# Transposed h stays on chip in freed operand sets during the last gate product; row scales by halves of the tokens; other places for loads

## The chip, the cores and the metric

The kernel runs on one core of one Trainium2 chip. The metric is the time of one execution on the device in microseconds (us). The median of several executions is given, and one further execution is recorded by the hardware profiler.

## The reference, cut to what matters

```python
# x: 1 x 512 x 2048, all in float32; D_MODEL = 2048, PLE_DIM = 256
h = x
for i in range(2):
    xn = rms_norm(h, norm_pre[i])
    if i == 0:                       # layer AB: attention and a recurrent mix
        proj = xn @ ab_w_in[0]
        ...
        y = concat(...) @ ab_w_out[0]
    else:                            # layer C: gated MLP over chunks of tokens
        u, v, g = split(xn @ c_w_in[0], 3)
        oc = chunked_spatial_gating(u, v, c_ln_g, c_ln_b, c_w_s, c_b_s)   # gelu, layer norm, 16 groups
        y = (oc * silu(g)) @ c_w_out[0]
    h = h + rms_norm(y, norm_post[i])
    h = h + (p[i] @ ple_w_proj[i]) * sigmoid(h @ ple_w_gate[i])
return h
```

The change touches the second pass (i = 1): the mix of layer C in one place, and above all what follows c_w_out: the RMS norm of y, the product p @ ple_w_proj (the "filler") and the last gate product h @ ple_w_gate with the output behind it.

## The kernel before

Products in float32 are made of three matmuls on split operands (high times high, high times low, low times high). For each 128x512 piece of a weight, ScalarE (ACT) casts the high part `whi` (L1466), and VectorE (DVE) subtracts it to get the low part `wlo` (L1467); four buffers of each stand ahead of TensorE (PE).

From c_w_in on, the products use a scheme of seven half-sized products in place of eight (`seven`, with the weights made in `pieces`). A `Pair` stands for 1024 columns of the weight. In the gate product there are two, a (output blocks n = 0, 1) and b (n = 2, 3), and `FIRST` sets the order b1, a1, b2, a2, a5, a6, a3, a4, a7, b5, b6, b4, b7, b3. Each of these fourteen is eight ticks k of six matmuls (128x512), 48 in all. Each has an operand set made of sums of quarters of h: `s[1]` in xh0 and xh1 (called A11), and `SETS` gives the tiles of the others, so yl0 to yl7 for product 2, yl8 to yl15 for 5, xl for 6 and 3, yh for 7 and 4. A set is free once its products of both pairs are done.

Weights come on SP's DMA queue (`load` in `pieces`, L1417, 512 KB each) into eight piece buffers. Sums of two weight blocks are made by VectorE (L1425), or by a DMA that accumulates, issued by GpSimd (POOL; `grow`, L1421). Product 4 loads eight halves of 256 KB (L1459) and adds them on VectorE.

Around the products a clock counts ticks: `later(n, step)` hangs a step on the n-th tick from here, and a scheduler with priorities orders each engine's instructions. Each engine, SP's queue included, then runs its own in order.

In the mix of layer C, groups 0 to 15 each take back normed columns of v from the DRAM tile `vd` (write L1566, load L1589, tile `sq`, both on ACT's queue) and norm them on ACT (L1598). In c_w_out, `out_block` writes scaled copies of y (L1138) and their squares (L1141) and adds the squares of each half of the tokens, e = 0 or 1, into `accq[e]` on POOL (L1142; `accq[1]` is the tile rstdB). A matmul with ones sums them over partitions (L1220), and `row_rstd` makes the row scale with Ln and Exp (L369, L370) behind a load of their table (L367). `update(q, e)` (L1192, L1193) multiplies y by it and adds to h. `load` (L1156) brings h back from DRAM before.

The filler (L251 to L253, four groups of 24 matmuls) runs between c_w_out and the gate product. ACT copies its results (L1207) and writes them to the DRAM tile `pd` from ACT's own queue. `flip` transposes a block of h on TensorE (L1232, four transposes), copies it on ACT (L1234) and writes it to the DRAM tile `rd`. SP fetches pd (L1273) and rd (L1274) back for each output block, and `emit` makes the sigmoid (L1277), multiplies by pd's part (L1278), adds rd's (L1280) and writes the output (L1282).

Of the kernel before, what the change touches and what calls it, by code (L numbers as in the profile page):

```python
# [16 lines left out]
P = 128  # L17
# [78 lines left out]
class Pair:  # L96


    def __init__(self, W, c0, n, emit):
        self.W, self.c0, self.n, self.emit = W, c0, n, emit  # L100
        self.E, self.H, self.acc, self.R, self.done = {}, {}, {}, {}, set()


class Net:
# [911 lines left out]
    def run(self):  # L1016
        tc = self.tc
        with ExitStack() as ctx:
# [10 lines left out]
            self.pd, self.rd = (self.t(dp, [P, 4, D], n) for n in ("pd", "rd"))  # L1029
# [92 lines left out]
    def last_layer(self, cp, fs, turn, wp, ps):  # L1122
# [8 lines left out]
        def out_block(pr, m, n, src):  # L1131
# [7 lines left out]
            if seen[e]:  # L1139
                sq = self.t(wp, [P, T], "sq")  # L1140
                nc.scalar.activation(sq, src, AF.Square)  # L1141
                nc.gpsimd.tensor_tensor(accq[e], accq[e], sq, ALU.add)  # L1142
            else:
                nc.scalar.activation(accq[e], src, AF.Square)
            seen[e] = True

# [34 lines left out]
        steps += [(82, ple)]  # L1181
# [8 lines left out]
        def update(q, e):  # L1190
            r = self.rstdB[:, e * 256 : e * 256 + 256].unsqueeze(1).broadcast_to([P, 2, 256])
# [3 lines left out]
        def filler():  # L1195
            phi, plo = self.pops
            for g in range(4):
                if g == 1:
                    self.A11 = self.whole_set()
                for q in (2 * g - 2, 2 * g - 1) if g else ():  # L1200
                    update(q, 0)
                    if q < 4:
                        self.part(self.A11, q, H[q, 0])
                accs = self.dense_tm(i["ple_w_proj"][1], g * T, T, phi, plo, ps)
                for m in range(4):
                    pj = self.slot("xl", 4 * (g % 2) + m, F32)
                    nc.scalar.copy(pj, accs[m])  # L1207
                    nc.scalar.dma_start(self.pd[:, m, g * T : (g + 1) * T], pj)
                if g == 0:
                    yield  # L1210
            for q in (6, 7):
                update(q, 0)

        more = filler()
        next(more)
        with tc.high_priority(HP):
            pt = self.t(ps, [P, T], "mm")
            for e in range(2):
                for a in range(2):
                    nc.tensor.matmul(  # L1220
                        pt[:, e * 256 : e * 256 + 256], self.ones, accq[e][:, a * 256 : a * 256 + 256],
                        start=(a == 0), stop=(a == 1),
                    )
            self.row_rstd(pt, self.rstdB, self.last)
        for _ in more:
            pass

        def flip(g, m):
# [4 lines left out]
            o = self.slot("xl", g + 4 * m, F32) if m < 2 else self.t(wp, [P, T], ("sg", "sq")[m % 2])  # L1233
            nc.scalar.copy(o, pt)  # L1234
            nc.scalar.dma_start(self.rd[:, m, g * T : (g + 1) * T], o)

        s, sets, x2, s1, s24, s3, x22 = self.sums(H, wp, SETS)
        s[1] = self.A11
        for q in range(4):
            x2(q)  # L1240
        spare = [[], []]
# [6 lines left out]
        def early_spare():  # L1248
            for j in range(8):
                spare[j % 2].append(self.slot("yh", j, F32))  # L1250

        def late_spare():
            for j in range(2):
                tl = self.t(self.xp, [P, 4, T], f"xh{2 + j}")
                spare[j][:] = [tl[:, q, :] for q in range(4)]

        steps = [(1 + k, lambda g=g, m=m: flip(g, m)) for k, (g, m) in enumerate((g, m) for g in (2, 0, 3, 1) for m in (0, 1))]
        steps += [(2 + 4 * q, lambda q=q: late(q)) for q in range(4)]
        steps += [(16, early_spare)]
        steps += [(19 + 3 * q, lambda q=q: s24(q)) for q in range(4)]  # L1260
        steps += [(30 + k, lambda g=g, m=m: flip(g, m)) for k, (g, m) in enumerate((g, m) for g in (2, 0, 3, 1) for m in (2, 3))]
        steps += [(38 + q, lambda q=q: s3(q)) for q in range(4)]
        steps += [(43 + q, lambda q=q: x22(q)) for q in range(4)] + [(47, late_spare)]
        for n, step in steps:
            self.later(n, step)
        pj, res = {}, {}

        def fetch(n, ms):
            for m in ms:
                pj[n, m], res[n, m] = (x[0] for x in spare)  # L1270
                for x in spare:
                    x.append(x.pop(0))
                nc.sync.dma_start(pj[n, m], self.pd[:, m, n * T : (n + 1) * T])  # L1273
                nc.sync.dma_start(res[n, m], self.rd[:, m, n * T : (n + 1) * T])  # L1274
# [12 lines left out]
        order = FIRST(*pairs, (4, 7, 3))  # L1287

        def ahead(step):
            if step + 1 < len(order):  # L1290
                pr, prod, _ = order[step + 1]
                if prod == 2:
                    fetch(pr.n, (0, 1))
                elif prod == 3:
                    self.later(3, lambda: fetch(pr.n + 1, (0, 1)))
                elif prod == 7:
                    fetch(pr.n + 1, (2, 3))
# [684 lines left out]
```

## Time and profile before

| | us |
|---|---|
| runs | 2279.76, 2271.38, 2278.86 |
| median | 2278.86 |
| profiled execution | 2278.64 |
| its span | 2276.9 |
| TensorE busy in the span | 2218.1 (97%) |
| VectorE, ScalarE, GpSimd busy | 1559.8, 1271.3, 267.5 |

The span runs from the first to the last instruction that the profile shows; the execution's time is 1.7 us longer. Times in the profile's rows are from the span's start. In them c_w_in's part that matters lies at 1495 to 1546, the mix from about 1622, the end of c_w_out at 2054.5, the filler to 2081.4, the gate product from there to 2268.9, and the last outputs to 2276.9. Rows of a busy engine give its start, its length, the engine, the line, and in brackets its idle time and what ended it. Rows of waits give the total, the number and the longest.

### The profile page before, as it was taken

The numbers are of one execution on the slowest core, as the hardware profiler recorded it, in microseconds if no ns is written. First come the engines' busy times: TensorE is split into PE (matmuls) and PEld (weight loads), VectorE is DVE, ScalarE is ACT, GpSimd is POOL, SyncE is SP. The second block draws the span as 40 slices with busy tenths as digits, with TensorE's granted clock in tenths as the row PEclk, the third lists the DMA queues.
The fourth block names the chain that finished last, engine by engine and source line by source line (L and its number), as shares of the span: only waits on it lengthen the run. The fifth ranks groups of instructions, "written<-read, shape, count | busy, mean of one in ns | idle before, by whom it ended". The sixth has DMA issues, their size and how long they took to land.

```text
span 2276.9 us, 40608 instructions
## 1 busy us (share of the span) xinstructions
PE 2218.1 (97%) x15369; PEld 1842.4 (81%) x15369; DVE 1559.8 (69%) x3008; ACT 1271.3 (56%) x2594; POOL 267.5 (12%) x318
## 2 busy tenths in 40 slices
PE   8999999999999999999999999999999999998988
PEld 7878888888887888878888888878878779997766
DVE  8666667666643877872237448878688688877868
ACT  5455555555443777753244547546566667556644
POOL 2000010010100000000010112101111111321020
PEclk9999999999999999999999999999999999999999
DMA  7322232223234533343335436776867776687696
GB/s 232 91 78 73 69 86 81 73 67 84 75 98 134 163 101 98 102 149 97 98 102 165 133 119 165 194 202 162 202 181 188 200 182 162 159 222 238 196 253 187
DMA packets 299442, 322.19 MB, mean 142 GB/s; under 512 B 15677, under 2 KB 191454, under 8 KB 298222
## 3 DMA queue, kind: packets, MB, share of 16 engines
q1 hardware_dynamic: 250990, 255.62, 36.8%
q0 software_dynamic: 21760, 41.95, 10.7%
q10 hardware_dynamic: 26496, 22.03, 3.2%
q8 instruction: 121, 1.98, 0.4%
q14 instruction: 75, 0.61, 0.1%
HBM read 284.64 MB, written 34.90 MB: 140 GB/s over the span
## 4 chain that ended last, share of the span: by engine, by line
PE 77%; DVE 9%; DMA 8%; ACT 3%; issue 3%; SPq 0%; ACTq 0%; POOL 0%; DVEq 0%; POOLq 0%
PE mm L1502 22%; PE mm L210 11%; PE mm L212 10%; PE mm L211 10%; PE mm L992 4%; PE mm L994 4%; PE mm L993 4%; DVE wlo L1467 3%; DMA sq<-vd 2%; DVE rq L1425 1%; PE tm L548 1%; DMA half<-in_ple_w_gate_dram 1%; PE tm L569 1%; DMA rq<-in_ple_w_gate_dram 1%; DMA half<-in_c_w_in_dram 1%
## 5 line engine op out<-in xcount | busy, mean ns | idle before, releaser
L196 DVE TENSOR_TENSOR wlo<-raw,whi 128x512 fp32r<-128x512 f32 x400 | 284.5, 719 | 309.1 <-ACT whi L194 272.2
L194 ACT CAST whi<-raw 128x512 fp32r<-128x512 f32 x400 | 247.0, 619 | 346.2 <-PE mm L993 151.3
L211 PE MATMUL mm<-xl,whi 128*128 128x512 f32 x1056 | 415.4, 393 | 0.0
L210 PE MATMUL mm<-xh,whi 128*128 128x512 f32 x992 | 412.6, 416 | 0.0
L212 PE MATMUL mm<-xh,wlo 128*128 128x512 f32 x992 | 392.4, 396 | 0.0
L1466 ACT CAST whi<-rq 128x512 fp32r<-128x512 f32 x432 | 264.4, 620 | 208.7 <-PE mm L1502 126.1
L1467 DVE TENSOR_TENSOR wlo<-rq,whi 128x512 fp32r<-128x512 f32 x432 | 300.0, 705 | 109.8 <-ACT whi L1466 107.8
L211 PEld LDWEIGHTS mm<-xl,whi 128*128 128x128 f32 x1056 | 199.6, 189 | 32.3
L212 PEld LDWEIGHTS mm<-xh,wlo 128*128 128x128 f32 x992 | 186.6, 188 | 41.1
L210 PEld LDWEIGHTS mm<-xh,whi 128*128 128x128 f32 x992 | 187.4, 189 | 33.2
L1502 PE MATMUL mm<-whi,yh 128*128 128x512 f32 x512 | 163.5, 396 | 3.8 <-ACT whi L1466 3.8
L1502 PE MATMUL mm<-whi,xl 128*128 128x512 f32 x512 | 163.0, 394 | 2.8 <-ACT whi L1466 2.3
L1502 PE MATMUL mm<-whi,yl 128*128 128x512 f32 x512 | 163.4, 395 | 0.7 <-ACT whi L1466 0.7
L1502 PEld LDWEIGHTS mm<-whi,yh 128*128 128x128 f32 x512 | 97.4, 190 | 24.9 <-ACT whi L1466 4.6
L1502 PEld LDWEIGHTS mm<-whi,xl 128*128 128x128 f32 x512 | 96.9, 189 | 24.2 <-ACT whi L1466 3.1
L1502 PEld LDWEIGHTS mm<-whi,yl 128*128 128x128 f32 x512 | 97.1, 190 | 21.9 <-ACT whi L1466 1.5
L1467 DVE TENSOR_TENSOR wlo<-raw,whi 128x512 fp32r<-128x512 f32 x128 | 88.7, 698 | 32.6 <-ACT whi L1466 32.4
L1466 ACT CAST whi<-raw 128x512 fp32r<-128x512 f32 x128 | 78.5, 620 | 56.7 <-PE mm L1502 25.3
L1502 PE MATMUL mm<-wlo,yl 128*128 128x512 f32 x256 | 101.5, 396 | 8.8 <-DVE wlo L1467 8.8
L1502 PE MATMUL mm<-wlo,yh 128*128 128x512 f32 x256 | 101.6, 397 | 1.5 <-DVE wlo L1467 1.5
L1502 PE MATMUL mm<-wlo,xl 128*128 128x512 f32 x256 | 101.0, 394 | 1.9 <-DVE wlo L1467 1.9
L1502 PE MATMUL mm<-whi,xh 128*128 128x512 f32 x256 | 82.2, 398 | 2.8 <-ACT xl L1207 1.7
(518 smaller groups left out, 4680.8 us busy)
## 6 DMA issues: line engine op xcount, KB each, us to landing
raw<-in_ab_w_in_dram SPq DMA_DIRECT2D x128, 512.0 KB, 3.9
rq<-in_c_w_in_dram SPq DMA_DIRECT2D x50, 512.0 KB, 6.2
raw<-in_ple_w_gate_dram SPq DMA_DIRECT2D x42, 512.0 KB, 4.5
rq<-in_c_w_in_dram POOLq DMA_DIRECT2D x36, 512.0 KB, 8.0
raw<-in_ab_w_out_dram SPq DMA_DIRECT2D x32, 512.0 KB, 3.8
raw<-in_c_w_in_dram SPq DMA_DIRECT2D x26, 512.0 KB, 3.7
half<-in_c_w_in_dram SPq DMA_DIRECT2D x48, 256.0 KB, 3.4
rq<-in_c_w_out_dram SPq DMA_DIRECT2D x24, 512.0 KB, 13.0
```

What stands on the lines that cost most here:

```text
L194: nc.scalar.copy(hi[:, : m * n], src)
L196: self.weng.tensor_tensor(lo[:, : m * n], src, f(hi[:, : m * n]), ALU.subtract)
L210: nc.tensor.matmul(acc, hi, xhi[k], start=(k == 0), stop=False)
L211: nc.tensor.matmul(acc, hi, xlo[k], start=False, stop=False)
L212: nc.tensor.matmul(acc, lo, xhi[k], start=False, stop=(k == nk - 1))
L548: nc.tensor.matmul(px[dst, e, :], a[src, e, :], b[src, e, :], start=True, stop=True)
L992: nc.tensor.matmul(accs[j], hi[:, js], xhi[k], start=(k == 0), stop=False)
L993: nc.tensor.matmul(accs[j], hi[:, js], xlo[k], start=False, stop=False)
L994: nc.tensor.matmul(accs[j], lo[:, js], xhi[k], start=False, stop=(k == nk - 1))
L1466: nc.scalar.copy(hi, src)
L1467: nc.vector.tensor_tensor(lo, src, f(hi), ALU.subtract)
L1502: nc.tensor.matmul(o, x, y, start=(first and r == 0 and j == 0 and not a), stop=(r == 7 and j == 2), **more)
```

## The change

Five things are changed.

1. The DRAM tile rd is gone. The sixteen flips copy into tiles that products 1 and 2 have freed (xh0, xh1 and yl0 to yl7), and `emit` adds from there. They are also later: eight in b2 and a2, eight in a5, a6 and a3, where before eight stood in b1 and a1, and eight from a2 on.
2. The results of the filler go to pd on SP's queue, not ACT's, and are fetched in five groups at set ticks.
3. The row scale is made per half of the tokens: the first half within the last products of c_w_out (with a table load of its own), the second behind the first group of the filler. The updates of the first half, with the sums of operands that follow from them, partly stand in c_w_out now. Six of the additions of squares go from POOL to VectorE.
4. Product a4 takes its weights by four accumulating DMAs of 512 KB instead of eight half loads and eight additions.
5. In the mix, each load of `vn` (L1589 before, L1576 after) is tied to the latest weight cast.

The core of the diff:

```diff
+        def row_scale(e):
+            with tc.high_priority(HP):
+                pt = self.t(ps, [P, 256], "mm")
+                for a in range(2):
+                    nc.tensor.matmul(pt, self.ones, accq[e][:, a * 256 : a * 256 + 256], start=(a == 0), stop=(a == 1))
+                self.row_rstd(pt, accq[e][:, :256], self.last)
...
                 nc.scalar.activation(sq, src, AF.Square)
-                nc.gpsimd.tensor_tensor(accq[e], accq[e], sq, ALU.add)
+                eng = nc.vector if pr.n == 2 and n + e > 2 else nc.gpsimd
+                eng.tensor_tensor(accq[e], accq[e], sq, ALU.add)
...
-        steps += [(82, ple)]
+        steps += [(82, ple), (98, lambda: row_scale(0))]
...
         def update(q, e):
-            r = self.rstdB[:, e * 256 : e * 256 + 256].unsqueeze(1).broadcast_to([P, 2, 256])
+            r = accq[e][:, :256].unsqueeze(1).broadcast_to([P, 2, 256])
...
+        for g in range(4):
+            accs = self.dense_tm(i["ple_w_proj"][1], g * T, T, phi, plo, ps)
+            for q in (g, g + 4):
                 update(q, 0)
+            self.part(self.A11, g, H[g, 0])
+            for m in range(4):
+                pj = self.slot("xl", 4 * (g % 2) + m, F32)
+                nc.scalar.copy(pj, accs[m])
+                nc.sync.dma_start(self.pd[:, m, g * T : (g + 1) * T], pj)
+            x2(g)
+            if g == 0:
+                row_scale(1)
...
         def flip(g, m):
...
-            o = self.slot("xl", g + 4 * m, F32) if m < 2 else self.t(wp, [P, T], ("sg", "sq")[m % 2])
+            if m < 2:
+                if m == 0 and g % 2 == 0:
+                    self.fl = self.t(self.xp, [P, 4, T], f"xh{1 - g // 2}")
+                o = self.fl[:, g % 2 * 2 + m, :]
+            else:
+                o = self.slot("yl", 2 * g + m - 2, F32)
+            res[g, m] = o
             nc.scalar.copy(o, pt)
-            nc.scalar.dma_start(self.rd[:, m, g * T : (g + 1) * T], o)
...
+        def fetch(n, m, o):
+            pj[n, m] = o
+            nc.sync.dma_start(o, self.pd[:, m, n * T : (n + 1) * T])
+
+        def first_fetch(n):
+            for m in range(2):
+                fetch(n, m, self.t(self.wq, [P, T], f"half{m}") if n == 1 else self.slot("yh", 2 - n + m, F32))
+
+        def next_fetch():
+            for j, ns in enumerate(((1, 0), (3, 2))):
                 tl = self.t(self.xp, [P, 4, T], f"xh{2 + j}")
+                for k in range(4):
+                    fetch(ns[k // 2], 2 + k % 2, tl[:, k, :])
+
+        def last_fetch():
+            tl = self.t(self.xp, [P, 4, T], "xh2")
+            for m in range(2):
+                fetch(3, m, tl[:, m, :])
...
+        steps = [(1 + 6 * q, lambda q=q: late(q)) for q in range(4)]
+        for at, g, m in (
+            (17, 2, 0), (18, 2, 1), (20, 3, 0), (21, 3, 1), (23, 0, 0), (25, 0, 1), (27, 1, 0), (29, 1, 1),
+            (34, 2, 2), (36, 2, 3), (38, 0, 2), (40, 0, 3), (42, 1, 2), (44, 1, 3), (46, 3, 2), (48, 3, 3),
+        ):
+            steps.append((at, lambda g=g, m=m: flip(g, m)))
...
+        steps += [(5, lambda: first_fetch(2)), (14, lambda: first_fetch(0)), (36, lambda: first_fetch(1))]
+        steps += [(56, next_fetch), (90, last_fetch)]
...
+        pairs[0].whole = True
+        self.seven(FIRST(*pairs, (4, 7, 3)), Sets(nxt), ps)
...
+            elif pr.whole:
+                tl = done = pr.E.pop(j)
+                grow(tl, 1, 0, j)
...
-                    nc.scalar.copy(hi, src)
+                    self.cast = nc.scalar.copy(hi, src)
...
-                nc.scalar.dma_start(vn, self.vd[:, g])
+                with tc.issue_after(self.cast.ins):
+                    nc.scalar.dma_start(vn, self.vd[:, g])
```

In the places that follow, names ending in numbers are tiles, `whi`/`wlo` the split weights, `mm` PSUM tiles. The first place is TensorE in the filler. Before, the ones matmul for the second half stands within the filler's second group, behind 40 of its matmuls:

```order
L253 MATMUL mm_22617<-whi_22639,yl_4536_21953 128x512
L251 MATMUL mm_22618<-whi_22639,yl_4535_21952 128x512
L252 MATMUL mm_22618<-wlo_22640,yl_4535_21952 128x512
L1220 MATMUL mm_22599<-rstdB_12776,ones_119 128x256 x2
L251 MATMUL mm_22620<-whi_22623,yl_4531_21941 128x512
L252 MATMUL mm_22620<-wlo_22624,yl_4531_21941 128x512
L253 MATMUL mm_22620<-whi_22623,yl_4532_21942 128x512
```

After, it stands directly behind the filler's first group of 24:

```order
L251 MATMUL mm_22559<-whi_22578,yl_4534_21951 128x512
L252 MATMUL mm_22559<-wlo_22579,yl_4534_21951 128x512
L253 MATMUL mm_22559<-whi_22578,yl_4535_21952 128x512
L1152 MATMUL mm_22616<-rstdB_12775,ones_118 128x256 x2
L251 MATMUL mm_22622<-whi_22628,yl_4530_21940 128x512
L252 MATMUL mm_22622<-wlo_22629,yl_4530_21940 128x512
L253 MATMUL mm_22622<-whi_22628,yl_4531_21941 128x512
```

The sum of the second half has moved ahead of sixteen matmuls, and everything after it in the filler stands behind it.

The second place is SP's queue in the gate product, around the weights of b5 (the four 512 KB loads rq from ple_w_gate). Before, fetches of pd and rd and writes of the output stand between them:

```order
L1417 DMA rq_4988_23958<-in_ple_w_gate_dram 128x2x512
L1273 DMA xh_4922_23630<-pd_101 128x512
L1417 DMA rq_4993_23985<-in_ple_w_gate_dram 128x2x512
L1282 DMA out_dram<-xh_4923_23631 128x512
L1273 DMA xh_4922_23630<-pd_101 128x512
L1282 DMA out_dram<-xh_4923_23631 128x512
L1417 DMA rq_4998_24008<-in_ple_w_gate_dram 128x2x512
L1274 DMA xh_4923_23631<-rd_102 128x512 x2
L1417 DMA rq_5003_24031<-in_ple_w_gate_dram 128x2x512
```

After, eight fetches of pd stand together ahead of b5's weights, and a half load of b4 and two output writes between them:

```order
L1243 DMA xh_4932_23699<-pd_101 128x512 x4
L1243 DMA xh_4933_23704<-pd_101 128x512 x4
L1400 DMA rq_4972_23911<-in_ple_w_gate_dram 128x2x512
L1400 DMA rq_4977_23938<-in_ple_w_gate_dram 128x2x512
L1445 DMA half_5017_24108<-in_ple_w_gate_dram 128x512
L1280 DMA out_dram<-xh_4783_23144 128x512
L1400 DMA rq_4982_23961<-in_ple_w_gate_dram 128x2x512
L1280 DMA out_dram<-xh_4783_23144 128x512
L1400 DMA rq_4987_23984<-in_ple_w_gate_dram 128x2x512
```

The fetches of pd have moved ahead of the four weights, and those of rd are gone.

The third place is ACT in c_w_in. Before, the first two loads of v (`sq` from `vd`) stand among the weight casts, some fifty rows ahead of their norm (row L1598):

```order
L1466 CAST whi_16854<-rq_3440_16769 128x512
L1466 CAST whi_16864<-rq_3440_16769 128x512
L1589 DMA sq_17660<-vd_103 128x512
L1466 CAST whi_16890<-rq_3402_16603 128x512
L1589 DMA sq_17731<-vd_103 128x512
L1466 CAST whi_16900<-rq_3402_16603 128x512
L1466 CAST whi_16916<-rq_3407_16626 128x512
```

After, the first load stands some ninety rows later and two casts ahead of its norm (now L1585):

```order
L1452 CAST whi_17639<-rq_3521_17167 128x512
L1452 CAST whi_17649<-rq_3521_17167 128x512
L1576 DMA sq_17659<-vd_102 128x512
L1452 CAST whi_17667<-raw_17374 128x512
L1452 CAST whi_17677<-raw_17374 128x512
L1585 ACTIVATE sq_17659<-sq_17659,nb_15726,rv_15725 128x128 x3
L1452 CAST whi_17688<-raw_17397 128x512
```

The load has moved behind the writes of vd and close to its use.

More of the change, by code (lines that the diff above doesn't have):

```diff
@@ L99, in __init__ @@
     def __init__(self, W, c0, n, emit):
-        self.W, self.c0, self.n, self.emit = W, c0, n, emit
+        self.W, self.c0, self.n, self.emit, self.whole = W, c0, n, emit, False
         self.E, self.H, self.acc, self.R, self.done = {}, {}, {}, {}, set()
@@ L1028, in run @@
             self.hd = self.t(dp, [P, KT, T], "hd")
-            self.pd, self.rd = (self.t(dp, [P, 4, D], n) for n in ("pd", "rd"))
+            self.pd = self.t(dp, [P, 4, D], "pd")
             self.vd, self.yd2 = (self.t(dp, [P, c, 4, P], n) for n, c in (("vd", KT), ("yd2", 8)))
@@ L1190, in update @@
         def update(q, e):
-            r = self.rstdB[:, e * 256 : e * 256 + 256].unsqueeze(1).broadcast_to([P, 2, 256])
+            r = accq[e][:, :256].unsqueeze(1).broadcast_to([P, 2, 256])
             nc.vector.tensor_tensor(Y[q, e], Y[q, e], r, ALU.mult)
             nc.vector.tensor_tensor(H[q, e], H[q, e], Y[q, e], ALU.add)
[L1195 to L1211, printed above, removed]
-                update(q, 0)
[L1214 to L1226, printed above, removed]
+        self.A11 = self.whole_set()
+        nxt, _, x2, s1, s24, s3, x22 = self.sums(H, wp, SETS)
+        nxt[1] = self.A11
+        phi, plo = self.pops
+        for g in range(4):
+            accs = self.dense_tm(i["ple_w_proj"][1], g * T, T, phi, plo, ps)
+            for q in (g, g + 4):
+                update(q, 0)
+            self.part(self.A11, g, H[g, 0])
[6 more added lines that the diff above has]
+                row_scale(1)
+        pj, res = {}, {}
         def flip(g, m):
@@ L1232, in flip @@
                 nc.tensor.transpose(pt[:, j * P : (j + 1) * P], src, self.ident)
-            o = self.slot("xl", g + 4 * m, F32) if m < 2 else self.t(wp, [P, T], ("sg", "sq")[m % 2])
-            nc.scalar.copy(o, pt)
-            nc.scalar.dma_start(self.rd[:, m, g * T : (g + 1) * T], o)
[L1237 to L1241, printed above, removed]
+            if m < 2:
[5 more added lines that the diff above has]
+            res[g, m] = o
+            nc.scalar.copy(o, pt)
         def late(q):
@@ L1246, in late @@
             s1(q)
[L1248 to L1253, printed above, removed]
-                tl = self.t(self.xp, [P, 4, T], f"xh{2 + j}")
-                spare[j][:] = [tl[:, q, :] for q in range(4)]
-        steps = [(1 + k, lambda g=g, m=m: flip(g, m)) for k, (g, m) in enumerate((g, m) for g in (2, 0, 3, 1) for m in (0, 1))]
-        steps += [(2 + 4 * q, lambda q=q: late(q)) for q in range(4)]
@@ L1259, in last_layer @@
[L1259 to L1264, printed above, removed]
-            self.later(n, step)
[L1266 to L1274, printed above, removed]
+        def fetch(n, m, o):
+            pj[n, m] = o
+            nc.sync.dma_start(o, self.pd[:, m, n * T : (n + 1) * T])
@@ new lines, in last_layer @@
+        steps = [(1 + 6 * q, lambda q=q: late(q)) for q in range(4)]
[4 more added lines that the diff above has]
+            steps.append((at, lambda g=g, m=m: flip(g, m)))
+        steps += [(24 + 4 * q, lambda q=q: s24(q)) for q in range(4)]
+        steps += [(49 + q, lambda q=q: s3(q)) for q in range(4)]
@@ L1276, in emit @@
+        steps += [(53 + q // 2, lambda q=q: x22(q)) for q in range(4)]
+        steps += [(5, lambda: first_fetch(2)), (14, lambda: first_fetch(0)), (36, lambda: first_fetch(1))]
+        steps += [(56, next_fetch), (90, last_fetch)]
+        for n, step in sorted(steps, key=lambda x: x[0]):
+            self.later(n, step)
         def emit(pr, m, n, src):
@@ L1286, in last_layer @@
         pairs = [Pair(W, 2 * j * T, 2 * j, emit) for j in range(2)]
[L1287 to L1297, printed above, removed]
-                    if 4 in pr.done:
-                        fetch(pr.n, (2, 3))
-                elif prod == 4 and 7 in pr.done:
-                    fetch(pr.n, (2, 3))
-        self.seven(order, Sets(s), ps, ahead)
+        pairs[0].whole = True
+        self.seven(FIRST(*pairs, (4, 7, 3)), Sets(nxt), ps)
         self.clock += 100
```

## The prediction

> **What bounds the kernel now.** I read the busy times of the engines first, then the waits of TensorE, then windows cut at the borders of the products, and last the chain of work that ended last. The page of the profile:
>
> ```profile
> PE 2218.1 (97%) x15369; PEld 1842.4 (81%) x15369; DVE 1559.8 (69%) x3008; ACT 1271.3 (56%) x2594; POOL 267.5 (12%) x318
> ...
> q1 hardware_dynamic: 250990, 255.62, 36.8%
> q0 software_dynamic: 21760, 41.95, 10.7%
> ```
>
> TensorE is the bound over the whole span, and the number of matmuls stays the same. So the change can give only time in which TensorE idles or runs at a lowered clock near the places it touches. The windows show where that is (us, busy time and instructions of each engine, granted clock, DMA share, GB/s):
>
> ```profile
> 1494.90:1521.50 26.60, 22.39 (x97) 17.76 (x95) 19.57 (x33) 11.29 (x20) 4.81 (x4) 0.97 0.75 174
> 1521.50:1546.10 24.60, 24.52 (x96) 19.82 (x97) 15.25 (x25) 12.10 (x21) 0.83 (x1) 0.89 0.76 229
> 1622.30:1702.00 79.70, 76.27 (x331) 60.15 (x329) 64.35 (x106) 49.88 (x98) 13.77 (x15) 1.00 0.71 179
> 2008.00:2020.00 12.00, 10.18 (x72) 9.98 (x72) 11.11 (x15) 7.54 (x15) 3.65 (x3) 0.86 0.63 184
> 2020.00:2054.50 34.50, 34.50 (x290) 34.50 (x289) 21.83 (x32) 17.09 (x31) 7.46 (x6) 1.00 1.04 297
> 2054.50:2081.40 26.90, 24.11 (x106) 19.28 (x105) 18.78 (x31) 19.87 (x39) 5.58 (x4) 1.00 0.60 191
> 2081.40:2113.20 31.80, 27.39 (x128) 22.17 (x129) 27.38 (x45) 21.02 (x39) 4.82 (x4) 0.95 0.94 265
> 2147.80:2155.30 7.50, 3.58 (x17) 2.75 (x17) 7.09 (x12) 5.21 (x10) 0.00 (x0) 0.75 0.54 164
> 2202.10:2222.10 20.00, 13.82 (x48) 10.49 (x49) 12.69 (x18) 6.42 (x11) 4.81 (x4) 0.83 1.05 257
> 2258.00:2268.90 10.90, 10.90 (x50) 8.87 (x48) 10.90 (x19) 5.94 (x10) 0.00 (x0) 1.00 0.36 116
> ```
>
> The last row is product b3: 48 matmuls in 10.9 us, 0.227 us each at the full clock, with nothing lost. That is my measure for the others. From 2054.5, where c_w_out ends, the filler should take 96 x 0.227 = 21.8 us, the fourteen gate products 152.6, and sixteen flips of 0.44 (row below) 7.0. That makes 181.4 us of the 214.4 to 2268.9: 33 us are lost, and the windows name where. TensorE's waits from 2054 on, and what stood behind them:
>
> ```profile
> PE mm L1502 <- DVE wlo L1467: 8.6, 5, 5.7
> PE mm L1232 <- ACT xl L1234: 3.2, 1, 3.2
> PE mm L1232 <- ACT sg L1234: 2.2, 1, 2.2
> PE mm L1502 <- ACT xl L1207: 1.7, 1, 1.7
> PE mm L1232 <- ACT sq L1234: 1.7, 1, 1.7
> PE mm L1220 <- POOL rstdB L1142: 1.1, 1, 1.1
> ```
>
> The 8.6 us (in us, times, longest) are the end of a queue of transfers, as the chain tells (start, us):
>
> ```profile
> 2065.41 1.13 PE mm L1220 x4
> ...
> 2084.93 0.44 PE mm L1232 x4
> ...
> 2179.80 8.14 DMA xh<-rd
> ...
> 2191.15 5.12 DMA out_dram<-xh
> ...
> 2197.12 11.27 DMA rq<-in_ple_w_gate_dram
> ...
> 2208.96 7.56 DMA rq<-in_ple_w_gate_dram
> ```
>
> SP issues in order. The weights of b5 stand in its queue behind fetches of pd and rd, which wait for the output of the product before to leave the tiles. They go out at 2197.1 and 2209.0 and land late.
>
> **The change, part by part.**
>
> *1. The vn loads (c_w_in, group one).* Before, the first vn load stands in ACT's order 60 casts ahead of its use and waits for a vd write:
>
> ```profile
> 1511.74 0.37 ACTq L1566 DMA_DIRECT2D vd<-comb  x1
> 1520.48 0.34 ACTq L1589 DMA_DIRECT2D sq<-vd  x1
> 1520.91 0.62 ACT L1466 CAST whi<-rq 128x512 fp32r<-128x512 f32 x1 [7.57 <-DMA vd<-comb]
> ```
>
> ACT stood for 7.57 us with weight casts queued behind. The windows 1494.9 to 1546.1 hold 193 matmuls, 43.8 us, in 51.2: 7.4 lost, part as a gap, part as the clock of 0.89. After, this load comes far later, when the write has landed; I take -7. The price is that the first loads are now issued two casts ahead of the norm, as the others were:
>
> ```profile
> ACT sq L1598 <- DMA sq<-vd: 17.4, 5, 5.4
> ```
>
> Five such waits stand beside 79.7 - 331 x 0.227 = 4.6 us lost in 1622.3 to 1702.0, near 0.9 each; two more make +1.7. Term: **-5.3** (ends: -7.4, and +2 if the wait moves to a later load).
>
> *2. Row scales by halves (filler).* The second half of the tokens now has its sum on TensorE after 24 matmuls of the filler instead of 40, that is at 2054.5 + 24 x 0.227 = 2060.0 on the old scale. What it needs is not there then:
>
> ```profile
> 2053.34 0.69 DVE L1528 TENSOR_TENSOR comb<-comb,comb 128x512 f32<-128x512 f32 x1
> ...
> 2062.03 1.28 ACT L367 ACT_TABLE_LOAD   x1
> 2063.32 0.63 ACT L1141 ACTIVATE sq<-comb 128x512 f32<-128x512 f32 x1
> 2064.09 1.26 POOL L1142 TENSOR_TENSOR rstdB<-rstdB,sq 128x512 f32<-128x512 f32 x1 [1.96 <-ACT sq L1141]
> ```
>
> The last square ends at 2063.95, still behind a table load. The add after it goes from POOL's 1.26 to VectorE's 0.69, but three more casts of operands (0.62 each) now stand among ACT's rows there, of which I count about one as late: the sum is ready near 2065.5. TensorE, which runs in order, stands 5.5 us with the rest of the filler behind it, against 1.1 before (the sum then started at 2065.41). The nearest gaps of that length are those in the rows 1494.9/1521.5 (a loss of 7.4 around a wait of ACT) and 2202.1 (clock 0.83); both pull the clock down behind them, at 2.75 us in the row 1521.5 (24.6 - 96 x 0.227 = 2.8). Against that, the 1.7 us for copies L1207 are likely absorbed by the earlier stall. 4.4 + 2.8 - 1.7 - 1 for a phase of the clock that may spare it: **+4.5** (ends -1.1, the wait gone, and +7.2). The extra table load (1.28) and Ln/Exp of the first half lie in c_w_out's last products, the row 2020.0:2054.5: ACT has 17.4 us free there and hides them. The twelve updates and two differences moved there take 0.69 each on VectorE, 9.7 us of the 12.7 that the row leaves free; without that cover they would delay the subtractions that TensorE waits for, by up to 9.7.
>
> *3. b1 and a1.* 31.8 us for 96 matmuls (21.8), eight flips (3.5), and 6.5 lost: VectorE is busy 27.38 of 31.8. Twelve updates and two sums are gone from here and the flips too. I leave 1 us: 22.8, **-9.0** (ends -10 and -4, if b1's weights come late). The flips return in b2, a2, a5, a6, a3: **+3.5**; their copies (0.58, row below) are ACT's, which has room.
>
> *4. rd, and the rest to b3.* From 2113.2 to 2268.9 stand 155.7 us, against twelve products (130.8) and eight flips (3.5): 21.4 lost. Of it the row 2147.8:2155.3 holds about 6, flips that waited for tiles which writes to rd still held:
>
> ```profile
> 2157.55 0.58 ACT L1234 COPY sg<-mm 128x512 f32<-128x512 f32 x1 [2.69 <-DMA rd<-sq]
> ```
>
> These writes don't exist any more. The row 2202.1:2222.1 (b5, 48 matmuls in 20.0) holds 9.1. Gone are 32 transfers of 256 KB, 8.4 MB (the sixteen flips written to rd and read back). q1 moved 255.62 MB in 36.8% of 2276.9 us, 305 MB per ms, so that is 27.5 us of all engines. a4 by accumulation takes four transfers of 512 KB through q0 (41.95 MB in 10.7%: 172 MB per ms): 12.2 us instead of 6.9, +5.3, and eight adds (0.69) leave VectorE. Net 22 us of DMA time out of a stretch of some 140, where the share runs from 0.54 to 1.05; b5's weights stand behind fewer fetches. I leave b5 2 us, b4's half loads 2.5, the flips 0.5, the rest 1: 6 lost, **-15.4** (ends: -20, and -4 if b5 and b6 stay as they are).
>
> The tail after the last matmul (2268.9 to 2276.9) is untouched.
>
> Sum: -5.3 + 4.5 - 9.0 + 3.5 - 15.4 = -21.7. Span 2276.9 - 21.7 = 2255.2; the profiled execution's time is 1.7 above its span, so 2257. That execution (2278.64) lies 0.2 under the median of the three runs: no correction. About 0.5%, 11.4 us, is what a measurement of this kernel can tell from no change.
>
> *A rule beside this.* The row 2008.0:2020.0 shows the clock at 0.86 behind a gap of 12.00 - 10.18 = 1.8 us: short gaps cost twice here, and I count so in the 6 us left. The Trainium skill, "TensorE: Matmul & The Clock Gate" (Why this matters for your kernels), says to allow no idle gaps over some 3 us, since a whole idle window halves the clock; that row disagrees. By the page the small gaps left would cost only themselves, and the sum would be about 2 us lower, 2255.
>
> **The rivals.**
>
> *Hidden anyway.* If b5's loads were late for their share of the DMA engines and not for their place in the queue, b5 keeps its 9.1 instead of 2: 7 more, 2264. For it: the DMA share of 1.05 there, and that a4's loads become dearer just ahead of b5. Against: the removed traffic is more than four times what accumulation adds.
>
> *Weights behind pd writes.* The sixteen pd writes move from ACT's queue to SP's, where a weight load for b1 (k 2 and 3) and all of a1's stand behind them. SP then waits for each copy of the filler, and a fetch of pd waits for a write to land:
>
> ```profile
> SPq L1273 <- DVE comb L1278: 24.2, 4, 15.0
> SPq L1274 <- DMA out_dram<-xh: 18.2, 7, 4.0
> ...
> SPq L1273 <- DMA pd<-xl: 4.4, 2, 2.8
> ```
>
> A load of gate weights takes 4.5 us from issue to landing (the page's last column):
>
> ```profile
> raw<-in_ple_w_gate_dram SPq DMA_DIRECT2D x42, 512.0 KB, 4.5
> ```
>
> b1's load goes out near 2078 and lands 4.5 later, against a use near 2086: some 4 us of cover. If the copies slip by more than that, b1 and a1 each lose about 4 and the clock behind it, and the gain of part 3 is gone: 2257 + 9, and with the upper end of part 2 (+2.7) and a1's second pair late by another 3.4, 2272, no change that can be told. The Trainium skill, "DMA: Bandwidth & Descriptors" (Issuing engines are not separate DMA queues), says that the queue of issue changes only the sequencer's time and not the engines that carry the data; by it the move gives no bandwidth, and the order on SP is all that it changes. The waits above agree.
>
> *Fetches hold SP (slower).* The three groups of pd fetches in the gate product each wait for their tiles to come free. Before, one such wait took 15.0 us (24.2 in four). Weights stand about a product ahead: 10.9 - 4.5 - 1.3 for cast and subtraction = 5.1 us of cover. Three holds of 15.0 would cost 3 x (15.0 - 5.1 + 2.8 for the clock) = 38: 2295. It decides from 13.9 us a hold on; below that the gain is smaller but stays. Against: two of the groups go to tiles that are long free.
>
> *All goes.* Neither the clock in part 2 nor b5's 2 us: 2247.
>
> **How the numbers follow.** The forecast, 2257 with its own range of 2250 to 2264: 0.45. All goes (2247): 0.10. Hidden anyway (2264): 0.22. Weights behind pd writes (2272): 0.15. Fetches hold SP (2295): 0.08. The first three are faster by over 0.5% (below 2267.5), 0.77; the fourth within 0.5%, 0.15; the last slower, 0.08. The range from 2245 to 2273 leaves out the slow one and part of the edges.
>
> **What would show it.** Right: no wait of ACT on vd<-comb and a clock near 1.00 after 1517; one wait of TensorE on the ones matmul of the second row scale of about 5.5 us and a lowered clock behind it; b1 and a1 together 22 to 24 us; no wait of the flips; b5 in 11 to 13 us. Wrong: SP's wait on copies of the filler with b1's weights landing after their casts were due; b5 at 20 us again with a DMA share over 1; a wait on the ones of under 2 us would say that ACT's squares were not the late part; several waits of over 10 us of SP on tiles for pd would put it on the slow side.

## The result, and the profile after

The changed kernel takes 2253.62 us (median of four runs, 2249.0 to 2256.05) against 2276.47 for the one before in the same comparison: a ratio of 0.990 with a 95% interval of 0.987 to 0.993. The forecast was 2257 us. The profiled execution has a span of 2254.3 us, 22.6 less than before.

The page of the profile after:

```profile
PE 2211.8 (98%) x15369; PEld 1839.4 (82%) x15369; DVE 1556.7 (69%) x3006; ACT 1274.5 (57%) x2597; POOL 264.1 (12%) x316
...
q1 hardware_dynamic: 249838, 253.52, 36.6%
q0 software_dynamic: 22848, 44.05, 11.3%
q10 hardware_dynamic: 21888, 13.64, 2.1%
```

The number of matmuls is the same, and only idle time between them went. The 8.4 MB of rd left two queues, its writes q10 (ACT's) and its reads q1 (SP's): in the run with part 1 alone each falls by 4.2 MB. Here q10 fell by 8.4 MB, from 22.03, because the writes of pd, another 4.2 MB, moved to q1; and the 2.1 MB of a4's half loads moved from q1 to q0.

Windows of the changed kernel at the borders of its stages (the columns as before):

```profile
1488.00:1515.00 27.00, 26.74 (x118) 21.61 (x117) 24.92 (x40) 14.74 (x25) 3.74 (x4) 1.00 0.56 146
1515.00:1540.00 25.00, 25.00 (x112) 20.71 (x111) 16.00 (x27) 12.52 (x21) 2.28 (x2) 1.00 0.91 258
1805.00:1848.00 43.00, 38.33 (x158) 30.13 (x157) 35.18 (x58) 24.43 (x50) 6.56 (x7) 0.92 0.67 173
2048.60:2080.20 31.60, 25.77 (x102) 20.77 (x101) 29.53 (x49) 23.94 (x46) 0.00 (x0) 0.89 0.61 204
2080.20:2101.90 21.70, 21.70 (x98) 17.91 (x97) 21.11 (x35) 16.31 (x30) 4.82 (x4) 1.00 0.91 238
2185.70:2198.20 12.50, 12.08 (x50) 8.78 (x49) 9.37 (x14) 5.61 (x10) 3.61 (x3) 1.00 1.08 233
2198.20:2213.70 15.50, 12.77 (x50) 9.79 (x49) 11.77 (x20) 5.39 (x9) 1.20 (x1) 0.89 0.74 167
```

The first two rows are c_w_in at the writes of vd: next to no idle time (0.26 us) and a clock of 1.00, where before it was 0.89. The third is the mix, which still loses. The fourth is the filler, longer than before, with the clock at 0.89. The fifth is b1 and a1: next to nothing is lost. The last two are b5, near its 10.9, and b6, which took over a part of the loss.

TensorE's waits from c_w_in to the end:

```profile
PE mm L1488 <- DVE wlo L1453: 10.2, 14, 2.3
PE mm L1152 <- issue: 5.8, 1, 5.8
PE mm L1607 <- DVE sg L1601: 2.4, 2, 1.9
```

No wait on a flip is left, and one new wait of 5.8 us on the ones matmul of a row scale (L1152) has come. Measured by the starts of the matmuls, the stages took (us; the end of c_w_out, which is the filler's first matmul, on the clock of each execution, then lengths):

| | before | after | part 1 alone | late scale |
|---|---|---|---|---|
| c_w_out ends at | 2054.6 | 2048.5 | 2050.7 | 2043.7 |
| filler | 26.9 | 31.5 | 27.5 | 23.5 |
| b1, a1 | 31.8 | 22.1 | 22.3 | 22.1 |
| b2, a2 | 23.1 | 25.3 | 25.3 | 25.3 |
| a5, a6, a3 | 42.4 | 36.5 | 36.5 | 36.5 |
| a4, a7 | 23.5 | 21.8 | 25.7 | 21.8 |
| b5, b6 | 32.6 | 28.0 | 23.3 | 26.6 |
| b4, b7, b3 | 34.2 | 32.7 | 34.8 | 33.3 |
| from the last matmul to the end | 7.9 | 7.8 | 8.0 | 8.1 |

The last two columns are kernels of the next section.

### The profile page after: what moved, and what is told of

It is laid out like the page before. It is cut to its first block, busy times and chain, and to the rows that moved or that the text cites. A ratio compares the mean times of both kernels' runs of the same rounds, so it can differ in the third digit from the quotient of the medians.

```text
span 2254.3 us, 40541 instructions
## 1 busy us (share of the span) xinstructions
PE 2211.8 (98%) x15369; PEld 1839.4 (82%) x15369; DVE 1556.7 (69%) x3006; ACT 1274.5 (57%) x2597; POOL 264.1 (12%) x316
## 3 DMA queue, kind: packets, MB, share of 16 engines
q0 software_dynamic: 22848, 44.05, 11.3%
## 4 chain that ended last, share of the span: by engine, by line
PE 78%; DVE 9%; DMA 6%; ACT 4%; issue 3%; SPq 0%; ACTq 0%; DVEq 0%; POOLq 0%
PE mm L1488 21%; PE mm L210 11%; PE mm L212 10%; PE mm L211 10%; PE mm L992 4%; PE mm L994 4%; PE mm L993 4%; DVE wlo L1453 3%; DMA sq<-vd 2%; PE tm L548 1%; ACT whi L1452 1%; DMA rq<-in_ple_w_gate_dram 1%; DVE rq L1408 1%; PE tm L569 1%; DMA gz<-gd 1%
## 5 line engine op out<-in xcount | busy, mean ns | idle before, releaser
L1453 DVE TENSOR_TENSOR wlo<-rq,whi 128x512 fp32r<-128x512 f32 x432 | 298.4, 700 | 103.0 <-ACT whi L1452 101.2
L1488 PEld LDWEIGHTS mm<-whi,xl 128*128 128x128 f32 x512 | 98.0, 191 | 23.5 <-ACT whi L1452 2.1
L1453 DVE TENSOR_TENSOR wlo<-raw,whi 128x512 fp32r<-128x512 f32 x128 | 89.0, 697 | 33.6 <-ACT whi L1452 33.2
```

What stands on the lines that cost most here:

```text
L1453: nc.vector.tensor_tensor(lo, src, f(hi), ALU.subtract)
L1488: nc.tensor.matmul(o, x, y, start=(first and r == 0 and j == 0 and not a), stop=(r == 7 and j == 2), **more)
```

## The experiments

**The loads of v alone.** The kernel before with this edit:

```diff
-                    nc.scalar.copy(hi, src)
+                    self.cast = nc.scalar.copy(hi, src)
...
-                nc.scalar.dma_start(vn, self.vd[:, g])
+                with tc.issue_after(self.cast.ins):
+                    nc.scalar.dma_start(vn, self.vd[:, g])
```

> The kernel before with part 5 alone (the loads of v tied to the latest weight cast). My theory: ACT's wait of 7.57 us on the write of vd is what c_w_in lost near 1517; it goes, the half clock behind it too, and the short loads cost 1 to 2 us, so c_w_out ends 4 to 7 us earlier than at 2054.5 and the whole is 2270 to 2273. Nothing after c_w_out changes. Rival: the gain before c_w_out came from other things in the changed kernel (the gap of 2.1 us near 2012, which c_w_out's new order closes); then c_w_out ends less than 3 us earlier.

Measured: 2267.97 us, a ratio of 0.996 (0.994 to 0.997), so 9.6 us less with an interval of 6 to 13, below the 2270 to 2273 that were named. The stretch of c_w_in at the write of vd, 51.2 us before (the windows 1494.9 to 1546.1), takes 43.6 us here and 43.6 to 44.4 in the ten other kernels with the edit (47.9 in part 1 alone, which has no edit there). So 6.8 to 7.6 us are won at that place, as the theory says. In this profile c_w_out ends at 2042.5, 12.1 earlier; the rest comes in the mix, where a small loss was expected. That is not steady: the changed kernel and seven of the kernels below, whose instructions up to there are alike, end c_w_out anywhere from 2042.5 to 2051.6 in their profiles, 2046.6 on average, and the two profiles without the edit at 2054.6 and 2050.7. So the edit is worth some 6 us by the average of the profiles and 9.6 by this run's times; the size is not shown more closely.

**The transposed blocks alone.** The kernel before, with the flips at the changed kernel's ticks and into the freed tiles, and rd gone. The sums of operands for later products (`s3`, `x22`) and the spare tiles also move to later ticks (from 38, 43 and 47 to 49, 53 and 56), so the run does not part the tiles from the ticks. All else is as before; of the edit this is the part at the flips and the fetches:

```diff
-            o = self.slot("xl", g + 4 * m, F32) if m < 2 else self.t(wp, [P, T], ("sg", "sq")[m % 2])
+            if m < 2:
+                if m == 0 and g % 2 == 0:
+                    self.fl = self.t(self.xp, [P, 4, T], f"xh{1 - g // 2}")
+                o = self.fl[:, g % 2 * 2 + m, :]
+            else:
+                o = self.slot("yl", 2 * g + m - 2, F32)
+            res[g, m] = o
             nc.scalar.copy(o, pt)
-            nc.scalar.dma_start(self.rd[:, m, g * T : (g + 1) * T], o)
...
-                nc.sync.dma_start(res[n, m], self.rd[:, m, n * T : (n + 1) * T])
```

> The kernel before with part 1 alone: flips go to the freed tiles of products 1 and 2 at the changed kernel's ticks, no rd, pd still written from ACT and fetched as before, row scales, a4 and the loads of v as before. My theory: the waits of the flips (6 us) and b5's late weights (9.1) go, the filler stays at 26.9, b1 and a1 lose the flips (31.8 to about 28) but stay bound by VectorE with the updates: total 13 to 18 us less, 2259 to 2264. Rival (hidden anyway): b5 stays at 18 us or more because the DMA engines and not SP's order made its weights late: total 5 to 9 us less, 2268 or more.

Measured: 2261.33 us, a ratio of 0.993 (0.991 to 0.995), so the total is what the theory gave. Two readings behind it were off. The gate product's fourteen products take 167.9 us instead of 187.6, a gain of 19.7, more than the median shows; and b1 and a1 are at 22.3, not 28. The windows of b1 with a1, and of b5 (2187.9 to 2198.8), in this kernel:

```profile
2078.20:2100.50 22.30, 22.29 (x100) 18.43 (x101) 22.30 (x38) 16.82 (x31) 4.81 (x4) 1.00 0.95 259
...
2187.90:2198.80 10.90, 10.90 (x49) 9.01 (x48) 10.57 (x16) 5.47 (x9) 3.67 (x4) 1.00 1.10 260
```

VectorE is busy in all of the 22.30 us, with fifteen of the nineteen update instructions of before still there, and TensorE loses next to nothing: a full VectorE was not what bound b1 and a1. And b5 runs at its 10.9 us although the DMA share is 1.10: a share over 1 does not by itself make it late. Whether it was rd's place in SP's queue or its bytes that made b5 late before, this run does not part.

What TensorE waited for in b1 and a1 is in the trace of before, on ACT:

```profile
2096.49 1.66 ACT L970 CAST yl<-xh 128x512 fp32r<-128x512 f32 x3
2098.05 1.07 ACT L1234 COPY xl<-mm 128x512 f32<-128x512 f32 x2
...
2099.81 0.62 ACT L970 CAST yl<-sg 128x512 fp32r<-128x512 f32 x1 [0.69 <-DVE yl L971]
2100.33 1.06 ACT L1234 COPY xl<-mm 128x512 f32<-128x512 f32 x2
```

The copies of the flips stand in ACT's order behind casts (L970 above all). The flips, and with them all matmuls behind them on TensorE, wait for these copies (the 3.2 us on L1234 among the waits of before), and the clock is halved from 2100.4 on. By these rows little of that wait comes from VectorE: ahead of the first copies the casts stand back to back, and only one behind them waits 0.69 us for VectorE (L971). Without flips there, nothing on TensorE waits for these copies.

**The second row scale later.** The changed kernel with

```diff
-            if g == 0:
+            if g == 1:
                 row_scale(1)
```

> The changed kernel with the second row scale behind the second group of the filler (48 matmuls) instead of the first (24). My theory: the 6.2 us gap of TensorE in the filler is the wait for the squares, and the half clock of 6.8 us behind it follows from it; both go, the filler takes 24 to 26 us instead of 31.6, b1 and a1 stay under 24, so 2246 to 2249. Rival: VectorE's updates of the second half are then late in b1 and a1, which give back 4 us or more: 2250 to 2254.

Measured: 2242.71 us, a ratio of 0.9855 to the kernel before (0.983 to 0.987), faster than both kernels. The filler's window:

```profile
2043.60:2067.10 23.50, 22.95 (x102) 18.76 (x102) 23.03 (x39) 22.44 (x45) 0.00 (x0) 1.00 0.65 225
```

23.5 us and a clock of 1.00, 8.0 less than in the changed kernel; b1 and a1 stay at 22.2. Both the filler and the total lie a little below what was named. So the changed kernel's early row scale cost 8 us, 6 as a gap and 2 by the clock behind it, and nothing in the products behind it needed it early. (The median fell by more, by 11; in the profile c_w_out ended 5 us earlier, which is within the scatter above.)

**Both row scales inside the filler.** The changed kernel with the first row scale behind the filler's first group, the second behind its second, the first half's updates back in the filler, and the differences of operands (`x2`) behind its last group; of the edit:

```diff
-        steps += [(82, ple), (98, lambda: row_scale(0))]
+        steps += [(82, ple)]
...
-            for q in (g, g + 4):
+            for q in ((), (0, 4, 1), (5, 2, 6), (3, 7))[g]:
                 update(q, 0)
...
-            if g == 0:
-                row_scale(1)
+            if g < 2:
+                row_scale(g)
```

> The changed kernel with both row scales inside the filler (the first half's behind the first group, the second's behind the second), and the updates of the first half and their sums back in the filler. If moving the updates into c_w_out is what made b1 and a1 short (32 to 21.7 us), they take 25 us or more here and the whole is 2250 to 2254. If the flips' leaving alone did it, b1 and a1 stay under 23 and the whole is as with the second row scale late, 2246 to 2249.

Measured: 2253.42 us, a ratio of 0.989 (0.987 to 0.991). The window of b1 and a1:

```profile
2075.50:2097.60 22.10, 22.10 (x102) 18.31 (x101) 21.93 (x37) 14.79 (x26) 4.81 (x4) 1.00 0.98 275
```

They take 22.1 us with twelve update instructions still in them, so the flips' leaving made them short and not the updates' leaving: that side of the expectation holds in the stage. The total it named does not: the filler takes 25.7 instead of 23.5, b5 15.8 instead of 12.2, and c_w_out ended at 2049.7 in the profile, within its scatter. Moving the first half's scale and updates into c_w_out is worth about 2 us in the filler. Behind b5's other 3.6 stands a late transfer: the eight fetches of pd go out at 2155.1 to 2159.5, in a3 (in the changed kernel at 2142.4 to 2155.0, in a6 and a3's start), the last plain load of b5's weights leaves 13.1 us ahead of b5 instead of 14.7, and the last accumulating one lands 11.3 us after b5's start instead of 8.0. Why the fetches get so late is not shown.

**The traffic put back without the order.** The changed kernel with sixteen writes more:

```diff
+        def ghost(g, m):
+            nc.scalar.dma_start(self.rd[:, m, g * T : (g + 1) * T], res[g, m])
+
+        steps += [(52 + 4 * g + m, lambda g=g, m=m: ghost(g, m)) for g in range(4) for m in range(4)]
```

> The changed kernel, which also writes each of its sixteen transposed blocks (256 KB) once to a DRAM tile that nobody reads, from ACT's queue in the products a6 to a7. It puts 4.2 MB back (13.8 us of all engines by q1's 305 MB per ms), without the waits and the order that rd had on SP. Theory (the DMA engines are the limit in a6 to b6, where the share is 1.04 to 1.11): b5 and b6 together lose 6 us or more on top of 28.0, total 2260 or more. Rival (SP's order was what made b5 late before, and the traffic alone costs nothing): b5 and b6 within 2 us, total within 3 of the changed kernel.

Measured: 2257.14 us, a ratio of 0.990 (0.989 to 0.992), where the changed kernel has the same 0.990. b5 takes 16.1 (12.5 in the changed kernel) and b6 15.0 (15.5): 3.1 us more, between the 6 and the 2 that were named. But the writes did not go where they were meant to. In the trace ten of the sixteen are issued in b2, a2 and a5 (2108.4 to 2137.9), where the DMA share is 0.37 to 0.81, five in a6 and a3 (2140.7 to 2152.8), and one in a4 (2169.1). So six of them, 1.6 MB, stand near b5's weights; at q1's 305 MB per ms that is 5.2 us of all engines (an estimate), against the 3.1 us that b5 and b6 lost. rd's reads, another 4.2 MB, were not put back at all. The run shows that bytes ahead of b5 cost something; how much of rd's cost was bytes, and how much its waits and its place in the queues, stays open.

**a4 with half loads again.** `pairs[0].whole = True` taken out of the changed kernel.

> The changed kernel with part 4 undone: a4 takes eight half loads and eight additions on VectorE again instead of four accumulating transfers. Theory: the part only moves a loss; a4 gets slower by 3 to 4 us (14.8 in the kernel with rd gone alone against 10.9), and b5 and b6, relieved of 5.3 us of transfers, get 4 to 5 us faster, so the total is within 3 us of the changed kernel. Rival: accumulation is a clear gain; b5 and b6 stay at 28 and the total is 4 us more.

Measured: 2267.58 us, a ratio of 0.995 (0.993 to 0.997); by its stages it is 14 us slower than the changed kernel, which neither side expected. b5 takes 10.9 and b6 12.4 here, 4.7 less, as expected, but a3 takes 18.1 and a4 21.4. The chain of this kernel:

```profile
2158.82 4.02 DMA half<-in_ple_w_gate_dram
2163.59 4.09 DMA half<-in_ple_w_gate_dram
2168.42 3.57 DMA half<-in_ple_w_gate_dram
2172.74 7.19 DMA half<-in_ple_w_gate_dram
```

The changed kernel parks two blocks of pd in the tiles half0 and half1 (`first_fetch(1)`) until a3's output is made. The half loads of a4 need these tiles, so the first of them can go out only at 2158.8, when a4 should begin, and then one pair after the other. Part 4 is what makes part 2's use of these tiles possible. That by itself it only moves some 4 us from a4 to b5 and b6 is read from two kernels that differ in other parts too (in the table, part 1 alone against after: 25.7 and 21.8, 23.3 and 28.0), and no run shows it alone.

**pd written from ACT's queue again.** `nc.scalar.dma_start(self.pd[...], pj)` in the changed kernel.

> The changed kernel with the writes of pd on ACT's queue, as before, instead of SP's. Theory: the queue that issues them is worth nothing here, since the weights of b1 and a1 came in time behind them; filler, b1 and a1 within 1 us, total within 3. Rival: the writes' issues (0.4 us each of ACT) stand behind the table load in the filler and ACT's copies get later, so the filler takes 2 us or more longer.

Measured: 2251.35 us, a ratio of 0.988 (0.986 to 0.990): no difference from the changed kernel's 0.990. The filler takes 30.1 (31.5 in the changed kernel, a little more apart than the 1 us named), b1 and a1 22.1. Both queues do here.

**A fetch of pd later, by the late row scale.** The kernel with the late row scale, with the second half of `next_fetch` at tick 87 behind b6's weights:

```diff
-        steps += [(56, next_fetch), (90, last_fetch)]
+        steps += [(56, lambda: next_fetch(0)), (87, lambda: next_fetch(1)), (90, last_fetch)]
...
-            nc.sync.dma_start(view(tl), block(*where))
+            self.came = nc.sync.dma_start(view(tl), block(*where))
...
+                with tc.issue_after(self.came.ins):
+                    fetch(ns[k // 2], 2 + k % 2, tl[:, k, :])
```

> The changed kernel with the second row scale behind the filler's second group, and the four fetches of pd for b's last outputs moved from ahead of b5's weights to behind b6's (1 MB later, 3.4 us of all engines). Theory (traffic limits a6 to b6): b5 and b6 together go from 26.6 to 24 or less, and the total is 2 to 3 us under the one with the late row scale alone: 2240. Rival: a single transfer's long landing behind accumulation, not the bytes, makes b6 late; then b5 and b6 stay at 26 and the total at 2243.

Measured: 2243.71 us, a ratio of 0.985 (0.983 to 0.987). b5 takes 12.6 and b6 14.0, together 26.6 as without the edit. The rival's number holds: with the second four fetches at 2178.0 to 2181.8, behind b6's weights and some 40 us after the first four instead of 11, b5 and b6 take the same time together. What makes b6 late is not what the rival said; it stands on VectorE in the changed kernel:

```profile
2202.69 0.68 DVE L1453 TENSOR_TENSOR wlo<-rq,whi 128x512 fp32r<-128x512 f32 x1
2206.26 0.69 DVE L1408 TENSOR_TENSOR rq<-rq,half 128x512 f32<-128x512 f32 x1 [2.88 <-DMA half<-in_ple_w_gate_dram]
2206.87 0.68 DVE L1453 TENSOR_TENSOR wlo<-rq,whi 128x512 fp32r<-128x512 f32 x1
```

An addition for b4 (L1408), which is not due for another product, stands in VectorE's order ahead of b6's subtraction (L1453) and waits 2.88 us for its half load.

**No half loads at all.** The kernel with the late row scale and `pairs[0].whole = pairs[1].whole = True`.

> The changed kernel with the late second row scale, and with b4 taking its weights by accumulating transfers too (no half loads or additions are left in the gate product). Theory: b6 is late because VectorE, in its order, waits 2.9 us for b4's half load ahead of the subtractions of b6; without it b6 goes from 14.4 to 12.5 or less and b4 stays at 10.9 to 11.5: 2239 to 2241. Rival: the dearer accumulation of 2 MB makes b4 late itself, 14 us or more, as the half loads did: 2245 or more.

Measured: 2243.09 us, a ratio of 0.9845 (0.982 to 0.987). b6 takes 12.0 instead of 14.4, and b4 12.7 instead of 11.5; from b5 to b4 it is 36.1 us instead of 38.1. So the waiting addition was b6's loss, and accumulation gives a part back in b4. The 2 us of the stages are too few to show in the time, which is that of the late row scale alone (2242.71).

**The same with pd on ACT's queue.**

> The same with the writes of pd back on ACT's queue. Theory: the queue matters by less than 1 us when TensorE does not wait in the filler: filler 23.5 to 24.5, total within 2 us of the kernel before this one. Rival: SP's fetches and weights go out earlier without the writes ahead of them, and the total falls by 2 us or more.

Measured: 2249.25 us, a ratio of 0.987 (0.983 to 0.990). Theory and rival both fail: the filler takes 25.5 instead of 23.5, with TensorE waiting 1.1 and 1.2 us for copies of the filler (L1214), and b5, b6 and b4 together 39.7 instead of 36.1. The intervals of the two kernels overlap, and each has one profile: that SP is the better queue when the filler is tight is likely, and not shown.

**The additions of squares back on POOL.** In the changed kernel:

```diff
-                eng = nc.vector if pr.n == 2 and n + e > 2 else nc.gpsimd
-                eng.tensor_tensor(accq[e], accq[e], sq, ALU.add)
+                nc.gpsimd.tensor_tensor(accq[e], accq[e], sq, ALU.add)
```

> The changed kernel with all additions of squares on POOL, as before; the second row scale stays early. Theory: the chain to the second row scale is the last square (late behind the table load) plus one addition, so TensorE's gap in the filler grows by the difference of one addition, 0.6 to 1.2 us, to about 7 us, and the filler takes 32 to 33 us. Rival: VectorE's queue, not the squares, held the additions; then the gap shrinks to 5 us or less.

Measured: 2255.47 us, a ratio of 0.989 (0.986 to 0.992). The filler takes 32.7, and the gap of TensorE grows from 6.2 to 8.0 us. What it waits for is now named:

```profile
PE mm L1151 <- POOL rstdB L1142: 7.6, 1, 7.6
```

The theory holds in kind; the step of 1.8 us is larger than the 0.6 to 1.2 named. POOL's last addition took 1.70 us here against VectorE's 0.69, which is 1.0 of it; the last square, too, ended 0.7 us later after the filler's start.

## Why the prediction was right, and where not

Term by term, against the profiles of before and after:

| term | forecast | measured |
|---|---|---|
| 1. loads of v, to the end of c_w_out | -5.3 | -6.1 |
| 2. row scales, filler | +4.5 | +4.7 |
| 3. b1 and a1 | -9.0 | -9.7 |
| flips in later products, and 4. the rest to b3 | -11.9 | -11.5 |
| tail | 0 | 0.0 |
| sum | -21.7 | -22.6 |

*Term 1* lies near the average of the profiles; one profile alone could have given anything from -3 to -12, and the run with this part alone gives -9.6 by its times, so that this profile's -6.1 lies so near is in part luck. The win at the write of vd is shown (-6.8 to -7.6, where -7 was forecast). The price of the short loads, +1.7, is not seen: a stretch of the mix that took 233.9 us before, and 235.8 in part 1 alone, took 227.3 to 237.5 in the eleven kernels with the edit, 231.8 on average. ACT's waits for vn went from 17.4 us in five to

```profile
ACT sq L1585 <- DMA sq<-vd: 18.2, 10, 5.1
```

in ten from c_w_in on: five more waits and not two, but 0.8 us more in all. The mix keeps a loss (the window 1805 to 1848 with its clock of 0.92).

*Term 2* held in size and mechanism. On the changed kernel's clock the filler starts at 2048.5 and the ones matmul at 2060.0, 11.5 us later, where 11.0 was worked out:

```profile
2057.22 1.28 ACT L367 ACT_TABLE_LOAD   x1
2058.52 0.63 ACT L1141 ACTIVATE sq<-comb 128x512 f32<-128x512 f32 x1
...
2059.18 0.69 DVE L1143 TENSOR_TENSOR rstdB<-rstdB,sq 128x512 f32<-128x512 f32 x1
```

The last square stands behind the table load, and the addition behind it, as read from the rows of before. The run with the late row scale shows that this is the whole of it. The size scatters: three other kernels with the same early row scale have the filler at 29.8, 30.1 and 30.9 us instead of 31.5.

*Term 3* had the right size for a wrong reason. The step that failed is "VectorE is busy 27.38 of 31.8", read as the bound. Of the 9.0 us, 3.5 were the flips' own matmuls; the other 5.5 I credited to the twelve updates and two sums that left these products. The runs with the transposed blocks alone and with both row scales in the filler show 22.3 and 22.1 us with updates left in place and VectorE busy nearly all of the time (22.30 and 21.93 us). TensorE's wait was for the flips' copies on ACT, and it went when the flips left. That they left in the same change is luck for the number.

*Term 4* is right in sum, and in part by luck: of the twelve products and sixteen flips 6.5 us are lost where 6 were left, but in other places. The flips' waits are gone. The row 2157.55, shown for them, starts behind their window, 2147.8 to 2155.3. Inside it two casts and a copy on ACT wait 0.5 to 0.6 us each for VectorE's sums, and the flips wait for copies in that order, as in b1 and a1; writes of rd did not hold them there. b5 lost 1.6 where 2 was left, b4 nothing where 2.5 was. But b6 lost 4.6, which was not forecast. Two runs with half loads in a4 have b6 at 12.4 us; with accumulation in a4 it is late, mostly by b4's waiting addition. The prediction had the dearer transfers in its balance of DMA time (+5.3) and did not carry them through to a product.

What is left in b5 follows one transfer. The fourth accumulating transfer of its weights lands 8.0 us after b5's start in the changed kernel (it takes 14.6), and b5 loses 1.6. In seven kernels made from the changed one it lands at 6.9 to 11.6, and the loss is each time what goes beyond 6.4: 1.3 for 7.7 with the late row scale, 4.9 for 11.3 with both scales in the filler, 5.2 for 11.6 with the extra traffic. In part 1 alone it lands at 5.0, and b5 loses nothing. The kernel with the later fetches (6.9, a loss of 1.7) does not fit.

*The rivals.* "Hidden anyway" fell with b5 at 10.9 us in the run with part 1 alone; but the extra traffic shows that bytes ahead of b5 are not free. "Weights behind pd writes" did not happen: b1 and a1 lost nothing, and with pd on ACT's queue the changed kernel's time is the same. The Trainium skill, "DMA: Bandwidth & Descriptors" (Issuing engines are not separate DMA queues), agrees with that run; the later pair of runs, 2249.25 and 2243.09, hints that the issuing engine's own time can count where it is tight. "Fetches hold SP" did not happen either. SP's longest waits for tiles to fetch pd into are

```profile
SPq L1243 <- DVE yh L971: 9.9, 2, 5.7
```

Two waits follow each other there: between the fetches of 2143.8 and 2153.2 SP stood for 9.1 us, 4.2 on VectorE and 4.7 on TensorE. That is below the 13.9 at which it would have decided, and TensorE lost nothing until b5.

*The rule beside it.* In the thirteen profiles from c_w_in on, gaps between two matmul starts of 1.5 to 1.85 us were followed by a window of half clock in 0 of 15 cases, gaps of 1.85 to 2.8 us in 23 of 40, and longer ones in 13 of 15. So counting short gaps twice was right about half of the time, and the 3 us of the Trainium skill, "TensorE: Matmul & The Clock Gate" (Why this matters for your kernels), is too high for this kernel.

## What to carry to other kernels

An engine that is full is a bound only if the one that sets the end waits for it: VectorE was busy for 27.4 of 31.8 us in b1 and a1 before, and for all of the time in a kernel that lost next to nothing there; what counted was what TensorE waited for, here copies of transposes standing behind casts in ACT's order. When a reduction is moved earlier on TensorE, work out from the rows when its last input is there; everything behind it waits until then, and the clock falls on top. A buffer borrowed for parking decides when its other user may start, so look at both edits as one.

## What the runs showed of the hardware that was not expected

Idle times of TensorE of under 2 us can already be followed by half its clock for a window of 3.4 us, and whether they are differs between executions of like instructions: the idle time of 1.8 us at the start of c_w_out (2.1 us between two matmul starts, near 2000 to 2012) was followed by half clock in the profiles of the kernel before, of the extra traffic and of pd on ACT's queue, and not in those of a4 with half loads and of the late row scale. Eight kernels with like instructions up to c_w_out's end reached it within 9 us of each other; the runs of one kernel lie 2 to 10 us apart.

TensorE ran b5 without loss while the DMA engines showed a share of 1.10 (part 1 alone), and lost 1.6 us at 1.08 (the changed kernel). The two differ in when the fourth accumulating transfer of b5's weights landed, 5.0 and 8.0 us after b5's start.
